# Hybrid attention / mLSTM step on one core: gate and up products of two FFN groups as float16 pairs

## The chip, the cores and the metric

The kernel runs on one core of one Trainium2 chip. The metric is the device time of one execution in microseconds; less is better. A core has five engines that run side by side, each through its own list in order: TensorE (PE, matmuls, with its weight loads shown as PEld), VectorE (DVE), ScalarE (ACT), GpSimd (POOL) and SyncE (SP, which here issues most DMA transfers). They wait for each other through semaphores. On-chip data lies in SBUF (128 partitions), sums of matmuls in the banks of PSUM.

## The reference

One layer over 1152 tokens (128 of a prompt, 1024 latent ones) of width 1024: grouped-query attention and a bidirectional mLSTM side by side, a joint output projection, then the part that is changed here, the feed-forward network (FFN):

```python
def swiglu(h, w_gu, w_down):
    g, u = jnp.split(h @ w_gu, 2, axis=-1)
    return (jax.nn.silu(g) * u) @ w_down
...
    h2 = rmsnorm(x, norm2_w) * (1 + sc2) + sh2
    x = x + g2 * swiglu(h2, w_gu, w_down)
```

`w_gu` is 1024 x 5632 (gate and up, 2816 columns each), `w_down` 2816 x 1024, all in float32. The shift `sh2`, scale `sc2` and gate `g2` come from a conditioning vector through `w_ada`.

## The kernel before

**Products of pairs.** A float32 product is made from three matmuls in a shorter format: each operand is split into an upper part (its rounding) and a lower part (what the rounding left), and high x high, high x low and low x high are summed in PSUM. The input projection `w_in` (class `Scaled`) does so with float16: since float16 has a small range, the operands are first multiplied by a power of two, found from a bound over all entries (`power_scale`: a PE transpose of a column of 128 bounds, a maximum on DVE, four small DVE operations on one number in `powers`, and a PE matmul that spreads the scale and its inverse to all partitions). The FFN and the output projection do it with fp32r, which needs no scale: `load_piece` (L139) loads 512 KB of weights into `raw` (two buffers), ACT casts the upper part into `whi` (L152), and `sub` (L137) makes the lower part `wlo` on DVE (five buffers each).

**Groups.** The 1152 tokens are nine blocks of 128, and the FFN runs over three groups of three blocks (384 tokens, `CT`), `c` = 0, 1, 2. In each, `gate_up` (L1316) goes over 4 or 5 of 22 column blocks `f`: for gate and for up it loads one weight piece, and `products` (L1310) makes 24 matmuls of 128 x 128 weights over 384 columns (8 steps of three, L1312 to L1314). From the two sums, `tn` = (tanh(g/2) + 1) u g on ACT and DVE (L1330 to L1332), which is split again into the pair `hl`. Then `down` (L1339) multiplies those by `w_down` in matmuls of 512 columns (L1112 to L1114) and adds to the rows `x1` (`add_gated`, L1098). The halving in the SiLU is folded into the gate `g2`.

**Beside the groups.** During groups 0 and 1, attention of the next group's blocks is woven in head by head: scores `S` (L1032, one buffer in PSUM), the row maximum on DVE (L1034), exp on ACT (L1035), a float16 pair of the probabilities (L1038, L1039), DMA transposes, and the products with the values (L1056, L1057). During the last `down` of a group, `norm2` (L1279) makes the pair `h2` = (`aTh`, `aTl`) of the next group: normalisation, PE transposes, scale and shift (L1301), a copy of the upper part (L1306) and `sub` for the lower one. The pair has one buffer each, b2 and b3, of six large ones.

**Order.** The loops write all instructions out once; a scheduler (`schedule_with_timeline_sim`) then orders them on each engine by its own simulated times. What the built program has in its lists is therefore not what the source order says. `prefill` (L1149), which runs ahead of group 0, adds the mLSTM half of the output projection to all rows; it waits for the rows `hm_d` that the last mLSTM head writes.

Of the kernel before, what the change touches and what calls it, by code (L numbers as in the profile page):

```python
# [8 lines left out]
F32 = mybir.dt.float32  # L9
F32R = mybir.dt.float32r  # L10
F16 = mybir.dt.float16
BF16 = mybir.dt.bfloat16
I32 = mybir.dt.int32
AF = mybir.ActivationFunctionType
ALU = mybir.AluOpType
# [4 lines left out]
P = 128  # L20
# [25 lines left out]
def hybrid_step(ctx: ExitStack, tc: tile.TileContext, I: dict, O: dict):  # L46
# [11 lines left out]
    def nm(s):  # L58
        uid[0] += 1
        return f"{s}_{uid[0]}"  # L60
# [10 lines left out]
    def emit(gen):  # L71
        for _ in gen:
            pass
# [62 lines left out]
    def sub(out, full, hi, eng):  # L136
        (dve if eng == "dve" else pool).tensor_tensor(out=out, in0=full, in1=hi, op=ALU.subtract)  # L137
# [28 lines left out]
    def power_scale(tp, one, bound, out):  # L166

        ps = bank()
        transpose(ps[0:1, 0:P], bound)
        v = tp.tile([1, 4], F32, name=nm("pv"), tag="pv", bufs=2)  # L170
        dve.tensor_reduce(out=v[:, 0:1], in_=ps[0:1, 0:P], axis=AX.X, op=ALU.max)
        powers(v, 1)
        yield
        ps = bank()
        mm(ps[:, 0:2], one, v[:, 2:4], start=True, stop=True)
        dve.tensor_copy(out, ps[:, 0:2])
        yield
# [55 lines left out]
    bcol = cp.tile([P, 48], F32, name="bcol")  # L233
    ncol = cp.tile([P, 16], F32, name="ncol")
    vsc = cp.tile([P, 4], F32, name="vsc")

    es_a = ExitStack()
    pA = es_a.enter_context(tc.tile_pool(name="pA", bufs=4, space=PSUM, reuse_waits="tile"))
# [835 lines left out]
    def a_tiles():  # L1074
        return (hp.tile([P, KD, CT], F32R, name=nm("aTh"), tag="b2"),
                hp.tile([P, KD, CT], F32R, name=nm("aTl"), tag="b3"))

    def new_x1(c):
        x1 = hp.tile([P, CB, D], F32, name=nm("x1"), tag=f"b{4 + c % 2}")
        for i in range(CB):  # L1080
            if c == 2:
                dma(x1[:, i, :], x1_d[i])
        return [x1[:, i, :] for i in range(CB)]
# [195 lines left out]
    def norm2(c, a, i):  # L1279

        x1 = a["x1"][i]
        if "h2" not in a:
            a["h2"] = a_tiles()
        th, tl = a["h2"]
        r = a["rs"][i]
        both = ap2.tile([P, KD, P], F32, name=nm("fl"), tag="pr", bufs=2)
        cnd = 0 if c * CB + i == 0 else 1
        for half in range(2):
            with hot(800):
                y = fp.tile([P, 512], F32, name=nm("y"), tag="y", bufs=2)  # L1290
                act(y, x1[:, half * 512 : (half + 1) * 512], AF.Copy, scale=r)
                ps = bank()
                for j in range(4):
                    transpose(ps[:, j * P : (j + 1) * P], y[:, j * P : (j + 1) * P])
                full = both[:, half * 4 : half * 4 + 4]
                for j in range(4):
                    k = half * 4 + j
                    if j == 0 and c == 0:
                        act(full[:, j, :], ps[:, j * P : (j + 1) * P], AF.Identity, scale=scale2[:, k, cnd : cnd + 1], bias=shift2[:, k, cnd : cnd + 1])
                        continue  # L1300
                    dve.tensor_scalar(  # L1301
                        out=full[:, j, :], in0=ps[:, j * P : (j + 1) * P],
                        scalar1=scale2[:, k, cnd : cnd + 1], scalar2=shift2[:, k, cnd : cnd + 1],
                        op0=ALU.mult, op1=ALU.add)
                oh = th[:, half * 4 : half * 4 + 4, i * P : (i + 1) * P]
                nc.scalar.copy(oh, full)  # L1306
                sub(tl[:, half * 4 : half * 4 + 4, i * P : (i + 1) * P], full, oh.bitcast(F32), "pool" if c == 0 else "dve")
            yield True

    def products(ps, wh, wl, th, tl):  # L1310
# [2 lines left out]
            mm(ps, wh[:, k, :], tl[:, k, :], start=False, stop=False)  # L1313
            mm(ps, wl[:, k, :], th[:, k, :], start=False, stop=(k == KD - 1))  # L1314

    def gate_up(a, f0, nf):  # L1316
        th, tl = a["h2"]
        acts = a["act"] = []
        for f in range(f0, f0 + nf):
            if True:  # L1320
                pg, pu = bank(), bank()
                for off, ps in ((0, pg), (D_FF, pu)):
                    src = w_gu[:, off + f * P : off + (f + 1) * P].rearrange("(k p) n -> p k n", p=P)
                    wh, wl = load_piece([(full_view, src)], (KD, P))
                    products(ps[:, 0:CT], wh, wl, th, tl)
                    yield 6
                parts = [(slice(0, CT), pg[:, 0:CT], pu[:, 0:CT])]
            tn = fp.tile([P, CT], F32, name=nm("tn"), tag="tn", bufs=2)
            for cs, g, u in parts:
                act(tn[:, cs], g, AF.Tanh, scale=0.5)  # L1330
                dve.scalar_tensor_tensor(out=tn[:, cs], in0=tn[:, cs], scalar=1.0, in1=u, op0=ALU.add, op1=ALU.mult)
                dve.tensor_tensor(out=tn[:, cs], in0=tn[:, cs], in1=g, op=ALU.mult)  # L1332
            hl = hlp.tile([P, 2, CT], F32R, name=nm("hl"), tag="hl", bufs=5)
            ah, al = hl[:, 0], hl[:, 1]
            nc.scalar.copy(ah, tn)  # L1335
            sub(al, tn, ah.bitcast(F32), "pool")
            acts.append((ah, al))
# [94 lines left out]
        ft.tile([P, 512], F32, name=f"lay_{tag}", tag=tag, bufs=bufs)  # L1432
    fp = ctx.enter_context(tc.tile_pool(name="fp", bufs=1, side="right", reuse_waits="tile"))

    cur, nxt = {}, {}
    cur["x1"], nxt["x1"] = new_x1(0), new_x1(1)
    es_x = ExitStack()
    xp = es_x.enter_context(tc.tile_pool(name="xp", bufs=1, side="right", reuse_waits="tile"))
    due = 0.0
# [8 lines left out]

    def groups(c, a, lst):
        for f0, nf in lst:  # L1450
            yield from gate_up(a, f0, nf)
            yield from down(c, a, f0, nf, 0)
            yield from down(c, a, f0, nf, 1)

# [10 lines left out]
    for c in range(NCH):  # L1465
        if c + 1 < NCH:
            main = groups(c, cur, GROUPS[:NG])
            for _ in range(4):
                next(main)
            weave(main, chain(previous(c, cur), att), 18 * sum(nf for _, nf in GROUPS[:NG]) - 24, 50)  # L1470
            emit(att)
            attn_out(nxt, oT, out_gates())
            emit(groups(c, cur, GROUPS[NG:-1]))
            f0, nf = GROUPS[-1]
            emit(gate_up(cur, f0, nf))
            n2 = chain(*[norm2(c + 1, nxt, i) for i in range(CB)])
            weave(chain(down(c, cur, f0, nf, 0), down(c, cur, f0, nf, 1)), n2, 6 * nf, 8)
            emit(n2)
            if c + 2 < NCH:
                oT = []  # L1480
                att = attention(c + 2, oT, set())
            nxt["prev"] = cur
            cur = nxt
            nxt = cur["next"] = {}
        else:
            main = groups(c, cur, LAST[:-1])
            for _ in range(4):
                next(main)
            weave(main, previous(c, cur), 24, 3)
            emit(main)  # L1490
            emit(gate_up(cur, *LAST[-1]))
            down_last(c, cur, *LAST[-1])


# [50 lines left out]
```

## Time and profile before

| | |
|---|---|
| median of three runs | 1588.04 us (1586.22 to 1590.58) |
| span of the profiled execution | 1590.3 us |
| PE busy | 1494.7 us (94%) |
| DVE busy | 1027.2 us (65%) |
| ACT busy | 768.8 us (48%) |
| POOL busy | 267.4 us (17%) |
| PE's mean granted clock | 0.978 |
| first and last gate/up product of group 0 | 632.9 and 933.1 us |
| of group 1 | 956.4 and 1278.6 us |
| of group 2 | 1301.9 and 1560.5 us |

The profile is of one execution. Its rows name the line, the engine, the operation, the output and the inputs with the program's names, shapes and types, the count, the busy time and the mean duration of one, and the idle time of the engine before them with what ended it. The profiler shows fp32r operands of PE as f32. PE's matmuls overlap each other, so their durations are longer than their distance; the distance is read from the starts in the timeline. The granted clock is a share of TensorE's full clock.

### The profile page before, as it was taken

The page shows a single profiled execution, that of the slowest core. Times are in us where ns is not written, and L with a number is a line of the kernel's source. Part 1 is how long each engine was busy: PE and PEld are TensorE (multiplying, and loading weights), DVE is VectorE, ACT ScalarE, POOL GpSimd, SP SyncE. Part 2 cuts the span into 40 slices and gives each one's busy share as a digit, 9 for nine tenths or more (in the row PEclk, how much of TensorE's full clock was granted, in tenths as well). Part 3 has the DMA queues.
Part 4 walks back from the last instruction along what each step waited for, and adds up shares of the span by engine and source line. Part 5 has one row for each costly group of instructions (what it writes and reads, how often), then busy time and mean ns, then how long its engine had stood idle before and what let it go on. Part 6 is the DMA issues. An engine that isn't in the chain of part 4 may idle for free.

```text
span 1590.3 us, 23425 instructions
## 1 busy us (share of the span) xinstructions
PE 1494.7 (94%) x8539; PEld 1249.4 (79%) x8539; DVE 1027.2 (65%) x2025; ACT 768.8 (48%) x1409; POOL 267.4 (17%) x357
## 2 busy tenths in 40 slices
PE   6799799999988679999999999999999999999996
PEld 3544467666766467888999999999898989999995
DVE  4778645755757576667654667877875575554555
ACT  4854365846656354535433435555552443323332
POOL 0023342332332243100110001000010101001111
PEclk9899899999999899999999999999999999999998
DMA  9474322432547746957754547968774445544441
GB/s 358 160 200 140 94 75 36 103 77 52 117 113 179 237 103 149 221 158 176 173 158 129 159 127 230 198 154 198 165 173 126 153 133 178 155 121 137 146 144 53
DMA packets 387881, 236.91 MB, mean 149 GB/s; under 512 B 170198, under 2 KB 346790, under 8 KB 387766
## 3 DMA queue, kind: packets, MB, share of 16 engines
q1 hardware_dynamic: 385110, 231.84, 54.0%
q10 hardware_dynamic: 2656, 3.58, 1.1%
q8 instruction: 67, 1.10, 0.3%
q14 instruction: 48, 0.39, 0.1%
HBM read 183.79 MB, written 13.26 MB: 124 GB/s over the span
## 4 chain that ended last, share of the span: by engine, by line
PE 75%; DVE 9%; DMA 8%; ACT 4%; issue 2%; SPq 1%; POOL 1%; ACTq 0%; DVEq 0%; POOLq 0%
PE mm L1313 11%; PE mm L1314 11%; PE mm L1312 11%; PE mm L1112 5%; PE mm L1113 5%; PE mm L1114 5%; PE S L1032 4%; PE wi L485 3%; PE wi L483 3%; PE wi L484 3%; PE mm L1144 1%; PE mm L1145 1%; DMA aw<-in_w_ada_dram 1%; PE po L1057 1%; PE po L1056 1%
## 5 line engine op out<-in xcount | busy, mean ns | idle before, releaser
L152 ACT CAST whi<-raw 128x1024 fp32r<-128x1024 f32 (+1 forms) x216 | 221.8, 1027 | 413.0 <-PE mm L1313 151.5
L137 DVE TENSOR_TENSOR wlo<-raw,whi 128x1024 fp32r<-128x1024 f32 (+1 forms) x216 | 260.5, 1206 | 203.8 <-ACT whi L152 203.2
L1313 PE MATMUL mm<-aTl,whi 128*128 128x384 f32 x1056 | 355.9, 337 | 2.7 <-DVE aTl L137 2.7
L1314 PE MATMUL mm<-aTh,wlo 128*128 128x384 f32 x1056 | 354.3, 335 | 0.0
L1312 PE MATMUL mm<-aTh,whi 128*128 128x384 f32 x1056 | 353.2, 336 | 0.0
L137 POOL TENSOR_TENSOR hl<-tn,hl 128x384 fp32r<-128x384 f32 x66 | 85.5, 1295 | 839.5 <-ACT hl L1335 721.3
L1313 PEld LDWEIGHTS mm<-aTl,whi 128*128 128x128 f32 x1056 | 198.5, 188 | 3.9 <-DVE aTl L137 3.3
L1312 PEld LDWEIGHTS mm<-aTh,whi 128*128 128x128 f32 x1056 | 198.1, 188 | 0.6
L1314 PEld LDWEIGHTS mm<-aTh,wlo 128*128 128x128 f32 x1056 | 198.4, 188 | 0.0
L1113 PE MATMUL mm<-wlo,hl 128*128 128x512 f32 x372 | 145.5, 392 | 0.0
L1112 PE MATMUL mm<-whi,hl 128*128 128x512 f32 x372 | 144.1, 392 | 0.0
L1114 PE MATMUL mm<-whi,hl 128*128 128x512 f32 x372 | 143.2, 392 | 0.0
L483 PE MATMUL wi<-ipair,hT 128*128 128x384 f16 (+2 forms) x408 | 136.2, 337 | 1.8 <-ACT hT L507 1.2
L484 PE MATMUL wi<-ipair,hT 128*128 128x384 f16 (+2 forms) x408 | 136.4, 337 | 0.0
L485 PE MATMUL wi<-ipair,hT 128*128 128x384 f16 (+2 forms) x408 | 132.5, 337 | 1.0 <-DVE hT L137 1.0
L1039 DVE SCALAR_TENSOR_TENSOR pl<-pr,st,ph 128x1152 f16<-128x1152 f32 (+1 forms) x72 | 93.8, 1303 | 33.8 <-ACT ph L1038 33.7
L1034 DVE TENSOR_REDUCE st<-S 128x1 f32<-128x1152 f32 (+1 forms) x72 | 88.9, 1235 | 14.6 <-PE S L1032 14.1
L1032 PE MATMUL S<-kst,qT 128*128 128x384 f32 (+1 forms) x400 | 87.6, 350 | 9.8 <-ACT pr L1035 5.6
L1035 ACT ACTIVATE pr<-S,st 128x1152 f32<-128x1152 f32 (+1 forms) x72 | 81.3, 1129 | 29.6 <-DVE st L1034 25.6
L1038 ACT ACTIVATE ph<-pr,st 128x1152 f16<-128x1152 f32 (+1 forms) x72 | 83.8, 1165 | 23.2 <-DVE st L1037 6.7
L1101 DVE TENSOR_TENSOR t<-mm,gl 128x512 f32<-128x512 f32 x102 | 68.9, 685 | 28.1 <-DMA gl<-g_d 10.2
L1032 PEld LDWEIGHTS S<-kst,qT 128*128 128x128 f32 x400 | 70.6, 191 | 14.7 <-ACT pr L1035 7.0
(366 smaller groups left out, 2539.7 us busy)
## 6 DMA issues: line engine op xcount, KB each, us to landing
raw<-in_w_gu_dram SPq DMA_DIRECT2D x132, 512.0 KB
raw<-in_w_down_dram SPq DMA_DIRECT2D x60, 512.0 KB
a<-in_w_ada_dram SPq DMA_DIRECT2D x24, 512.0 KB
gl<-g_d SPq DMA_DIRECT2D x36, 256.0 KB
aw<-in_w_ada_dram SPq DMA_DIRECT2D x16, 512.0 KB
iraw<-in_w_in_dram SPq DMA_DIRECT2D x32, 256.0 KB
raw<-in_w_out_dram SPq DMA_DIRECT2D x12, 512.0 KB
x<-in_x_sample_dram SPq DMA_DIRECT2D x11, 512.0 KB
```

The lines of the kernel that those rows point to most:

```text
L137: (dve if eng == "dve" else pool).tensor_tensor(out=out, in0=full, in1=hi, op=ALU.subtract)
L152: nc.scalar.copy(hi[:, :n], raw[:, :n])
L483: mm(ps[:, :n], ah, wh[:, k % 2, c0 : c0 + n], start=(k == 0), stop=False)
L484: mm(ps[:, :n], ah, wl[:, k % 2, c0 : c0 + n], start=False, stop=False)
L485: mm(ps[:, :n], al, wh[:, k % 2, c0 : c0 + n], start=False, stop=(k == KD - 1))
L1032: mm(S[:, n, 0:w], qT[:, h, :], kst[kv][:, t, c0 + n * w : c0 + (n + 1) * w], start=(t == 0), stop=(t == 1))
L1112: mm(ps, ah, wh[:, k % 2, :], start=(k == 0), stop=False)
L1113: mm(ps, ah, wl[:, k % 2, :], start=False, stop=False)
L1114: mm(ps, al, wh[:, k % 2, :], start=False, stop=(k == nk - 1))
L1312: mm(ps, wh[:, k, :], th[:, k, :], start=(k == 0), stop=False)
L1313: mm(ps, wh[:, k, :], tl[:, k, :], start=False, stop=False)
L1314: mm(ps, wl[:, k, :], th[:, k, :], start=False, stop=(k == KD - 1))
```

## The change

Group 0 stays with fp32r pairs. Groups 1 and 2 make gate and up from float16 pairs. Line numbers of the profile of before hold for the kernel before; the new functions are called by name.

- `bound_h2` (new, ahead of `prefill`) bounds |h2| by max|scale2| sqrt(1024) + max|shift2|, makes a power of two of it, and multiplies `scale2` and `shift2` by that for all three groups. `guc` holds the scales and inverses.
- `gate_piece` (new) loads a piece of `w_gu`. In group 0 it calls `load_piece` as before and sums |w| over each row of the piece on ACT (`AF.Abs` with an accumulator, 44 passes, its elementwise output `jg` is not used). In groups 1 and 2 it makes the float16 pair `wf`: ACT writes the upper half with the scale, DVE the lower one, both halves into one buffer, in turn of tag whi or wlo.
- `bound_w_gu` (new, behind the last `gate_up` of group 0) makes the power of two for `w_gu` from the largest row sum.
- The pair `h2` of groups 1 and 2 (`half_tiles`) takes one buffer, b3 for group 1 and b2 for group 2.
- tanh takes its scale, and the second gate operation the square of the inverse, from `guc`.
- The SBUF reserve for DMA descriptors is set to 256 bytes in a partition.

```diff
+    guc = cp.tile([P, 8], F32, name="guc")
+    gsum = cp.tile([P, 2 * NF], F32, name="gsum")
+    one2 = cp.tile([1, P], F32, name="one2")
+    dve.memset(one2, 1.0)
...
+    def half_tiles(c):
+        t = hp.tile([P, 2, KD, CT], F16, name=nm("hF"), tag=("b2", "b3")[c % 2])
+        return t[:, 0], t[:, 1]
...
-            a["h2"] = a_tiles()
+            a["h2"] = a_tiles() if c == 0 else half_tiles(c)
...
+    def gate_piece(c, i, src):
+        if c == 0:
+            raw = wp.tile([P, 1024], F32, name=nm("raw"), tag="raw", bufs=2)
+            jk = ft.tile([P, 1024], BF16, name=nm("jg"), tag="t2", bufs=3)
+            pieces = load_piece([(full_view, src)], (KD, P), raw=raw)
+            act(jk, raw, AF.Abs, accum_out=gsum[:, i : i + 1])
+            return pieces
+        raw = wp.tile([P, 1024], F32, name=nm("raw"), tag="raw", bufs=2)
+        w = wp.tile([P, 2, 1024], F16, name=nm("wf"), tag=("whi", "wlo")[i % 2], bufs=5)
+        dma(raw.rearrange("p (k n) -> p k n", k=KD), src)
+        hi, lo = w[:, 0], w[:, 1]
+        act(hi, raw, AF.Copy, scale=guc[:, 2:3])
+        dve.scalar_tensor_tensor(out=lo, in0=raw, scalar=guc[:, 2:3], in1=hi, op0=ALU.mult, op1=ALU.subtract)
+        return tuple(v.rearrange("p (k n) -> p k n", k=KD) for v in (hi, lo))
...
-                    wh, wl = load_piece([(full_view, src)], (KD, P))
+                    wh, wl = gate_piece(c, 2 * f + (off > 0), src)
...
-                act(tn[:, cs], g, AF.Tanh, scale=0.5)
+                act(tn[:, cs], g, AF.Tanh, scale=guc[:, 4:5])
...
-                dve.tensor_tensor(out=tn[:, cs], in0=tn[:, cs], in1=g, op=ALU.mult)
+                dve.scalar_tensor_tensor(out=tn[:, cs], in0=tn[:, cs], scalar=guc[:, 5:6], in1=g, op0=ALU.mult, op1=ALU.mult)
...
+    def bound_h2():
+        b2 = fp.tile([P, 2], F32, name="b2", tag="s1", bufs=3)
+        dve.tensor_reduce(out=b2[:, 0:1], in_=shift2, axis=AX.XY, op=ALU.max, apply_absolute_value=True)
+        dve.tensor_reduce(out=b2[:, 1:2], in_=scale2, axis=AX.XY, op=ALU.max, apply_absolute_value=True)
+        dve.scalar_tensor_tensor(out=b2[:, 1:2], in0=b2[:, 1:2], scalar=float(D) ** 0.5, in1=b2[:, 0:1], op0=ALU.mult, op1=ALU.add)
+        emit(power_scale(fp, one2, b2[:, 1:2], guc[:, 0:2]))
+        for t in (scale2, shift2):
+            dve.tensor_scalar(out=t, in0=t, scalar1=guc[:, 0:1], scalar2=None, op0=ALU.mult)
+        inverses_gu(guc[:, 1:2])
+    def inverses_gu(inv):
+        dve.tensor_scalar(out=guc[:, 4:5], in0=inv, scalar1=0.5, scalar2=None, op0=ALU.mult)
+        dve.tensor_tensor(out=guc[:, 5:6], in0=inv, in1=inv, op=ALU.mult)
+    def bound_w_gu():
+        b2 = fp.tile([P, 2], F32, name="b2w", tag="s1", bufs=3)
+        dve.tensor_reduce(out=b2[:, 0:1], in_=gsum, axis=AX.X, op=ALU.max)
+        emit(power_scale(fp, one2, b2[:, 0:1], guc[:, 2:4]))
+        dve.tensor_tensor(out=guc[:, 6:7], in0=guc[:, 1:2], in1=guc[:, 3:4], op=ALU.mult)
+        inverses_gu(guc[:, 6:7])
...
     cur["x1"], nxt["x1"] = new_x1(0), new_x1(1)
+    bound_h2()
...
-            emit(gate_up(cur, f0, nf))
+            emit(gate_up(c, cur, f0, nf))
+            if c == 0:
+                bound_w_gu()
...
-    nc = _bacc.Bacc("TRN2", target_bir_lowering=False, num_devices=1)
+    nc = _bacc.Bacc("TRN2", target_bir_lowering=False, num_devices=1, dynamic_dma_scratch_size=256)
```

More of the change, by code (lines that the diff above doesn't have):

```diff
@@ L1306, in norm2 @@
                 nc.scalar.copy(oh, full)
-                sub(tl[:, half * 4 : half * 4 + 4, i * P : (i + 1) * P], full, oh.bitcast(F32), "pool" if c == 0 else "dve")
+                sub(tl[:, half * 4 : half * 4 + 4, i * P : (i + 1) * P], full, oh.bitcast(F32) if c == 0 else oh, "pool" if c == 0 else "dve")
             yield True
@@ L1314, in products, with gate_up @@
             mm(ps, wl[:, k, :], th[:, k, :], start=False, stop=(k == KD - 1))
-    def gate_up(a, f0, nf):
+    def gate_piece(c, i, src):
[12 more added lines that the diff above has]
+        return tuple(v.rearrange("p (k n) -> p k n", k=KD) for v in (hi, lo))
+    def gate_up(c, a, f0, nf):
         th, tl = a["h2"]
@@ L1450, in groups @@
         for f0, nf in lst:
-            yield from gate_up(a, f0, nf)
+            yield from gate_up(c, a, f0, nf)
             yield from down(c, a, f0, nf, 0)
@@ L1490, in hybrid_step @@
             emit(main)
-            emit(gate_up(cur, *LAST[-1]))
+            emit(gate_up(c, cur, *LAST[-1]))
             down_last(c, cur, *LAST[-1])
```

## The prediction

> **What bounds the kernel now.** I read the busy times of five stretches first, then the list of PE's waits behind 632 us, where the FFN begins, then the timeline of PE for the pace of its matmuls.
>
> The columns after each stretch are its length, then busy time (and instructions) of PE, PEld, DVE, ACT and POOL, the granted clock, and the DMA share with GB/s:
>
> ```profile
> span 1590.3 us, 23425 instructions
> 200.00:500.00 300.00, 287.18 (x1863) 207.40 (x1862) 176.69 (x483) 191.34 (x539) 95.55 (x213) 0.98 0.41 88
> 632.00:956.00 324.00, 321.73 (x1751) 295.29 (x1750) 205.10 (x291) 139.97 (x183) 32.29 (x24) 1.00 0.61 163
> 956.00:1302.00 346.00, 344.96 (x1926) 318.04 (x1924) 256.28 (x379) 176.14 (x234) 27.29 (x22) 1.00 0.67 169
> 1302.00:1563.00 261.00, 259.37 (x1392) 245.84 (x1391) 140.53 (x185) 89.17 (x116) 28.41 (x22) 1.00 0.48 145
> 1563.00:1590.00 27.00, 14.22 (x63) 11.45 (x61) 16.98 (x54) 6.40 (x15) 4.67 (x4) 0.81 0.15 58
> ```
>
> The second, third and fourth rows are the three FFN groups. PE is busy for over 99% of each at full clock, while DVE stands at 63, 74 and 54% and ACT at 43, 51 and 34%. All of PE's waits from 632 us on:
>
> ```profile
> PE mm L1313 <- DVE aTl L137: 2.7, 2, 1.6
> PE po L1057 <- DMA plT<-pl: 1.3, 1, 1.3
> PE S L1032 <- ACT pr L1035: 1.0, 1, 1.0
> ```
>
> That is 5 us in 958. So PE bounds the FFN, and time that its matmuls give up there is time off the end, until something else is late.
>
> **Pace of the products.** First and last of 45 gate/up matmuls in a row (third group), then first and last of 24 float16 matmuls of the same 384 columns in the input projection. Columns: start, duration, line:
>
> ```profile
> 1399.82 0.33 PE L1312 MATMUL mm<-aTh,whi 128*128 128x384 f32 x1
> ...
> 1407.45 0.33 PE L1314 MATMUL mm<-aTh,wlo 128*128 128x384 f32 x1
> ...
> 316.30 0.33 PE L808 MATMUL wi<-hT,ipair 128*128 128x384 f16 x1
> ...
> 320.04 0.33 PE L810 MATMUL wi<-hT,ipair 128*128 128x384 f16 x1
> ```
>
> Durations overlap, so the starts count: 7.63 us over 44 steps is 173.4 ns; 3.74 us over 23 steps is 162.6 ns. Both stretches mix the three products in the same pattern. The weight loads under them and the matmuls by kind:
>
> ```profile
> L1312 PE MATMUL mm<-aTh,whi 128*128 128x384 f32 x1056 | 353.2, 336 | 0.0
> L1312 PEld LDWEIGHTS mm<-aTh,whi 128*128 128x128 f32 x1056 | 198.1, 188 | 0.6
> L808 PEld LDWEIGHTS <-ipair 128*128 128x128 f16 x96 | 10.1, 105 | 6.9 <-issue 2.2
> ```
>
> Each of the three products has 1056 matmuls, 352 a group, so the second and third group have 2112. All change. **Term 1: 2112 x (173.4 - 162.6) ns = 22.8 us less.**
>
> **A wait put between the first and second group.** `bound_w_gu` takes the maximum of the row sums: one PE transpose, a reduce on DVE, four small operations, one PE matmul that spreads the scale. In the built program's order PE has the transpose and this matmul directly behind the last gate/up product of the first group, ahead of the down products, and DVE has between them the last block's two gate operations and one lower half of a weight piece. Rows that price it:
>
> ```profile
> 933.50 0.56 DVE L1331 SCALAR_TENSOR_TENSOR tn<-tn,mm 128x384 f32<-128x384 f32 x1 [2.10 <-PE mm L1314]
> 934.09 0.55 DVE L1332 TENSOR_TENSOR tn<-tn,mm 128x384 f32<-128x384 f32 x1
> L171 DVE TENSOR_REDUCE pv<-mm 1x1 f32<-1x128 f32 x7 | 1.9, 277 | 4.2 <-PE mm L116 4.2
> L161 DVE TENSOR_SCALAR pv<-pv 1x1 f32<-1x1 f32 x7 | 1.0, 140 | 0.2
> L137 DVE TENSOR_TENSOR wlo<-raw,whi 128x1024 fp32r<-128x1024 f32 x204 | 252.3, 1237 | 183.7 <-ACT whi L152 183.1
> ```
>
> L1331 starts when the last product ends, at 933.50 in this trace; then 0.56 + 0.28 + 0.55 + 0.14 + 1.24 + 3 x 0.14 = 3.2 us, and 0.2 us from DVE to PE: PE stands for 3.4 us where it now goes on with the down products. Queued behind the waiting matmul are all of those. On DVE nothing is added ahead of the wait but the reduce. Such a stop can cost clock as well. Stretches with a long and a short wait in them, and what follows each:
>
> ```profile
> PE S L1032 <- DVE qT L137: 4.1, 1, 4.1
> 174.00:179.00 5.00, 0.91 (x6) 0.33 (x4) 3.83 (x13) 2.45 (x4) 0.00 (x0) 1.00 0.34 105
> 179.00:184.00 5.00, 4.95 (x21) 2.70 (x22) 3.11 (x8) 0.58 (x1) 3.06 (x2) 0.66 0.00 0
> 1302.00:1304.00 2.00, 0.53 (x4) 0.22 (x2) 2.00 (x3) 1.71 (x4) 0.00 (x0) 1.00 0.73 257
> 1304.00:1312.00 8.00, 7.83 (x45) 7.83 (x46) 7.11 (x20) 3.37 (x6) 0.00 (x0) 1.00 0.72 200
> 541.00:549.00 8.00, 6.85 (x18) 5.26 (x19) 3.25 (x4) 1.98 (x3) 0.00 (x0) 0.52 0.92 280
> PE mm L116 <- DMA t<-hm_d: 6.4, 1, 6.4
> ```
>
> After the 4.1 us wait the clock is 0.66 for 5 us (1.7 us lost); after 541 us, behind a wait of 6.4 us, 0.52 for 8 us (3.8 us lost); after the 1304 us stop of under 2 us, 1.00. The price lies between 0 and 3.8 us; I take 1.7, the nearest wait. **Term 2: +5.1 us, from 3.4 to 7.2.** The Trainium skill ("TensorE: Matmul & The Clock Gate", "Why this matters for your kernels") asks for no PE gaps over about 3 us between bursts, since one idle window halves the clock. The rows above bear it out; by that rule 3.4 us is at the edge, and without the clock loss the sum would be 1.7 us lower.
>
> **The scale of h2.** `bound_h2` stands ahead of the prefill: three DVE operations, a transpose, a reduce, four small ones, a matmul, a copy, two scalings of 16 columns, two of one column. PE's order puts its matmul ahead of the first transposes of the mLSTM rows, which wait for the load t<-hm_d today (the 6.4 us above). DVE also has one lower half of w_out in the chain. With L171 and L161 the DVE chain is some 2 us and that half 1.24, so between 0 (all under the load) and 3.3 us: PE's own matmuls there soon wait for the w_out pieces too. **Term 3: +1.5 us.** `dve.memset(one2)` is one row of 128 columns at the start, where PE waits for loads.
>
> **Row sums in the first group.** 44 ACT passes with their accumulator reads, priced by the same shape in the norm statistics, beside the passes that change:
>
> ```profile
> L1275 ACT ACTIVATE jk<-x 128x1024 bf16<-128x1024 f32 x15 | 15.8, 1054 | 2.7 <-DVE x L1102 1.8 <-POOL x L1102 0.8
> L1275 ACT ACTIVATION_READ_ACCUMULATOR jk<-x 128x1 f32 x15 | 2.8, 187 | 0.0
> L152 ACT CAST whi<-raw 128x1024 fp32r<-128x1024 f32 x204 | 214.3, 1051 | 379.5 <-PE mm L1313 138.6 <-DMA raw<-in_w_gu_dram 112.9 <-PE mm L1114 89.0
> L218 ACT ACTIVATE ipair<-iraw,isc 128x1024 f16<-128x1024 f32 x10 | 11.5, 1153 | 5.0 <-PE wi L485 4.9
> L219 DVE SCALAR_TENSOR_TENSOR ipair<-iraw,isc,ipair 128x1024 f16<-128x1024 f32 x10 | 13.0, 1304 | 6.4 <-ACT ipair L218 6.4
> L1035 ACT ACTIVATE pr<-S,st 128x1152 f32<-128x1152 f32 x64 | 78.4, 1225 | 22.7 <-DVE st L1034 21.9 <-DVE st L1037 0.3
> ```
>
> 44 x 1.241 = 54.6 us takes ACT from 140 to 195 us of 324 (60%): hidden behind PE on average. Not always: 12 heads of attention run in that stretch, one S buffer is freed by the exp on ACT, and a pass ahead of the exp delays the next head's S, with everything behind it on PE. From 0 to 12 x 1.24 = 14.9 us; PE waits 1.0 us for this now, so **Term 4: +2 us.** The junk output shares the t2 buffers with the gated adds, and a raw buffer is held one pass longer; the five weight buffers run ahead of PE and hide that.
>
> **Conversions in groups two and three.** Upper halves from 1.05 us (the cast, L152) to 1.153, lower ones from 1.237 to 1.304: 88 x 0.10 + 88 x 0.07 = 15 us over two engines with room. A pair takes half the buffer space, so more pieces lie ahead. The tight place is the second group: 24 heads, DVE 256 us, which becomes some 260 of 335 (78%). Bounds are 0 and 24 heads x half a lower half, 15.6 us; with DVE in no queue of PE's there now, **Term 5: +3 us.** The gate's second operation becomes a scalar_tensor_tensor, which L1331 shows at the same 0.55 us.
>
> **Order elsewhere.** The smaller descriptor reserve frees SBUF, and buffers that overlapped earlier ones no longer do: the built order moves the loads of the q/k tables ahead of eight loads of w_ada, and the key norms with them. The total of work is the same. The stretch in which they land:
>
> ```profile
> 100.00:200.00 100.00, 88.72 (x524) 45.09 (x523) 78.03 (x238) 43.36 (x86) 35.97 (x31) 0.93 0.44 134
> ```
>
> PE is idle there for 11 us, which a better order could win in part and a worse one add to; I take half on either side: **Term 6: 0, from -6 to +6 us.**
>
> **Sum.** -22.8 + 5.1 + 1.5 + 2 + 3 + 0 = -11.2 us. The profiled span of 1590.3 us lies 2.3 above the median of 1588.04; from the span it is 1579.1, from the median **1576.8**, forecast 1577. Its own range, by terms 2 to 6, is 1570 to 1583.
>
> **Rivals.**
> A, the gain whole: terms 3 to 5 hidden, the wait without loss of clock, 1588 - 22.8 + 3.4 = 1569, or a few less if the new order helps. For it: PE's 5 us of waits. Against: the fuller ACT and DVE. Chance 0.22.
> B, slower by the softmax chain: each S waits for an exp behind one ACT or DVE pass of about 1.2 us in more than the odd case. Of the 36 heads behind 632 us, 18 late ones cost 21.6 us: 1588 - 22.8 + 6.6 + 21.6 = 1593. It decides from 16.2 / 1.2 = 13 heads. For it: one S buffer, and the new program leaves only 5.3 us of PE work between some heads. Against: 1.0 us of such waits today. With half as many late heads it ends at 1583. Chance 0.14 for slower, 0.12 for the half.
> C, the pace stays: float16 streams no faster here, because something other than the weight load sets 173.4 ns. Then only terms 2 to 5 remain: 1588 + 11.6 = 1600. Against: the 162.6 ns over the same two streams. Chance 0.04.
> D, the weight load sets the pace: with 105 ns instead of 188 a matmul would come every 105 ns, 2112 x 68 ns = 144 us less, 1444. Against: the 162.6 ns with that very load. Chance 0.01. The Trainium skill (same page, "Back-to-back issue gap") gives about 131 ns for pairs of 512 columns; no row here shows it.
>
> **How the numbers follow.** The forecast has 0.47. What this kernel's measurement can tell from no change is 0.3%, 4.8 us, so faster means under 1583.3: forecast, A and D, 0.70. Within: the half of B and a part of the forecast's neighbours, 0.15. Slower: B and C with an unlucky term 6, 0.15. The range takes A with a good order (1563) and B (1593).
>
> **What would show it.** Starts of hF,wf products 162 to 163 ns apart; the second stretch shorter by 11 us less its new waits, the third group by 11.4; one PE wait of some 3.4 us for DVE pv just ahead of the down products of the first group, and the clock row behind it; PE S <- ACT pr summed from 632 us on, under 5 us. I am wrong if that last wait passes 15 us, if ACT whi waits turn into PE waits for pieces, or if the span before 632 us moves by over 6.

## The result, and the profile after

The changed kernel takes 1599.49 us (median of four runs, 1596.92 to 1601.65) against 1588.42 us for the kernel before beside it (1586.22 to 1590.58): a ratio of 1.0071, interval 1.0055 to 1.0087. That is 11.3 us slower, where 11.2 us faster was forecast, and outside the range. The profiled execution took 1599.78 us with a span of 1598.0 us.

Lengths by the first and the last gate/up product of each group, from the profiled executions:

| stretch | before, us | after, us | forecast of the difference |
|---|---|---|---|
| start to first product of group 0 | 632.9 | 621.3 | 1.5 (terms 3 and 6) |
| group 0 | 300.2 | 316.7 | 2 (term 4) |
| group 0 to 1 | 23.3 | 30.3 | 5.1 (term 2) |
| group 1 | 322.2 | 323.9 | -11.4 and a part of term 5 |
| group 1 to 2 | 23.3 | 24.2 | 0 |
| group 2 | 258.6 | 251.6 | -11.4 and a part of term 5 |
| behind it | 29.8 | 30.0 | 0 |

The differences add up to 7.7 us and not to 11.3, because the profiled execution of the kernel before was a long one: no other run of it on record has a span over 1589.9 us, and its own is 1590.3.

Some of the first two rows is only a shift: group 0 of the changed kernel holds 20 more matmuls of 512 columns (398 in place of 378), work of `prefill` that came later in the order. At 0.23 us each that is 4.7 us. So the start gained 7 us and group 0 lost 12. Busy times after, with the columns of the prediction's table of stretches:

```profile
621.00:938.00 317.00, 308.11 (x1658) 281.57 (x1657) 192.24 (x260) 178.19 (x258) 30.33 (x25) 0.99 0.61 160
938.00:968.00 30.00, 25.73 (x117) 20.72 (x117) 23.86 (x51) 14.19 (x19) 1.38 (x1) 0.94 0.41 123
968.00:1292.00 324.00, 315.48 (x1809) 220.76 (x1808) 234.85 (x337) 169.58 (x218) 24.88 (x21) 0.99 0.68 173
1316.00:1568.00 252.00, 247.81 (x1386) 163.94 (x1384) 141.10 (x185) 93.29 (x114) 24.26 (x21) 1.00 0.50 150
```

PE (its busy time against the length, first two numbers) idles 9 us in the first group, 4 in the step to the second, 8.5 in the second and 4 in the third; in the prediction's rows of the kernel before it was 5 us for all of them. In the second group DVE is busy for 72% and ACT for 52%, against 74 and 51% in the row of before: it isn't load that makes PE wait there. The longest of PE's waits from 621 us on, beside the list of the prediction (us in total, times, longest):

```profile
PE po L1060 <- DMA phT<-ph: 4.8, 4, 2.1
PE mm L175 <- DVE pv L164: 4.3, 1, 4.3
PE mm L1320 <- DVE tn L1355: 4.1, 2, 2.3
PE mm L1321 <- DVE hF L137: 3.0, 2, 2.3
PE mm L1322 <- DVE wlo L137: 2.8, 4, 0.8
PE S L1036 <- ACT pr L1039: 2.6, 4, 1.1
PE mm L1320 <- ACT whi L152: 2.1, 2, 1.7
```

The second row is the one that was forecast. The others are new or larger, and only 2.6 us of them are the softmax chain of rival B.

Short waits cost clock as well. In the prediction's rows of the kernel before, the clock is 1.00 in all three groups. The changed kernel has, beside the stretch behind the forecast wait (shown further down), three more at half clock:

```profile
642.90:646.30 3.40, 3.16 (x10) 3.16 (x11) 3.40 (x4) 3.40 (x5) 1.01 (x1) 0.50 0.54 153
987.70:991.10 3.40, 3.40 (x12) 1.64 (x11) 3.23 (x5) 0.73 (x3) 0.02 (x1) 0.50 0.88 275
1049.10:1052.50 3.40, 3.40 (x13) 2.54 (x10) 2.34 (x3) 1.03 (x1) 0.00 (x0) 0.50 0.86 211
```

They come at waits of 1.7 us (for whi, at 641.9 us), 2.3 us (for tn, at 987.2) and 2.1 us (for phT, at 1048.6). Each loses about 1.7 us, together some 5 us that no term of the prediction holds, and all three waits are shorter than the 3 us that it quotes as a limit. It isn't so behind every such wait: PE also waits 2.3 us for hF at 1319 us, and the clock stays full.

The pace of the float16 products came out as forecast. First and last of 240 in a row in the third group of the changed kernel (start, duration):

```profile
1380.88 0.34 PE L1320 MATMUL mm<-hF,wf 128*128 128x384 f16 x1
...
1419.73 0.33 PE L1322 MATMUL mm<-hF,wf 128*128 128x384 f16 x1
```

38.85 us over 239 steps is 162.6 ns. But products that the change doesn't touch became slower. First and last of 90 down products of 512 columns in the third group, before:

```profile
1407.62 0.39 PE L1112 MATMUL mm<-whi,hl 128*128 128x512 f32 x1
...
1427.84 0.39 PE L1114 MATMUL mm<-whi,hl 128*128 128x512 f32 x1
```

and the same products of the changed kernel:

```profile
1419.76 0.53 PE L1120 MATMUL mm<-whi,hl 128*128 128x512 f32 x1
...
1440.65 0.39 PE L1122 MATMUL mm<-whi,hl 128*128 128x512 f32 x1
```

20.22 us against 20.89 us over 89 steps, 227 against 235 ns. The three groups have 1188 of these. Some 0.1 us of the 0.67 is the first step behind float16 products; the rest, 6.4 ns a step, is no wait and no clock, since nearly all steps are longer and the median is 234 ns in each group, against 227. For 1188 products that is some 7.5 us.

### The profile page after: what moved, and what is told of

Read it like the earlier page. It is cut to its first block, busy times and chain, and to the rows that moved or that the text cites. A ratio compares the mean times of both kernels' runs of the same rounds, so it can differ in the third digit from the quotient of the medians.

```text
span 1598.0 us, 23425 instructions
## 1 busy us (share of the span) xinstructions
PE 1482.3 (93%) x8545; PEld 1094.3 (68%) x8545; DVE 1028.9 (64%) x2049; ACT 826.5 (52%) x1497; POOL 264.0 (17%) x357
## 5 line engine op out<-in xcount | busy, mean ns | idle before, releaser
L137 DVE TENSOR_TENSOR wlo<-raw,whi 128x1024 fp32r<-128x1024 f32 (+1 forms) x128 | 151.1, 1183 | 147.1 <-ACT whi L152 145.4
L1321 PE MATMUL mm<-hF,wf 128*128 128x384 f16 x704 | 230.5, 328 | 3.0 <-DVE hF L137 3.0
L1320 PE MATMUL mm<-hF,wf 128*128 128x384 f16 x704 | 229.3, 328 | 4.1 <-DVE tn L1355 4.1
L1322 PE MATMUL mm<-hF,wf 128*128 128x384 f16 x704 | 230.4, 328 | 0.0
L137 POOL TENSOR_TENSOR hl<-tn,hl 128x384 fp32r<-128x384 f32 x66 | 78.2, 1186 | 859.7 <-ACT hl L1359 791.4
L152 ACT CAST whi<-raw 128x1024 fp32r<-128x1024 f32 (+1 forms) x128 | 128.7, 1006 | 158.5 <-DMA raw<-in_w_down_dram 63.6
L1336 ACT ACTIVATE wf<-raw,guc 128x1024 f16<-128x1024 f32 x88 | 100.6, 1147 | 150.3 <-DMA raw<-in_w_gu_dram 132.4
L1337 DVE SCALAR_TENSOR_TENSOR wf<-raw,guc,wf 128x1024 f16<-128x1024 f32 x88 | 113.2, 1287 | 65.9 <-ACT wf L1336 65.6
L1322 PE MATMUL mm<-aTh,wlo 128*128 128x384 f32 x352 | 119.1, 339 | 2.8 <-DVE wlo L137 2.8
L1320 PE MATMUL mm<-aTh,whi 128*128 128x384 f32 x352 | 119.3, 339 | 2.1 <-ACT whi L152 2.1
L1321 PE MATMUL mm<-aTl,whi 128*128 128x384 f32 x352 | 118.6, 337 | 0.0
L1321 PEld LDWEIGHTS <-wf 128*128 128x128 f16 x704 | 69.2, 98 | 49.3 <-issue 6.1
L1322 PEld LDWEIGHTS <-wf 128*128 128x128 f16 x704 | 69.2, 98 | 48.6 <-issue 4.8
L1320 PEld LDWEIGHTS <-wf 128*128 128x128 f16 x704 | 69.1, 98 | 47.0 <-issue 2.9
```

What stands on the lines that cost most here:

```text
L152: nc.scalar.copy(hi[:, :n], raw[:, :n])
L1320: mm(ps, wh[:, k, :], th[:, k, :], start=(k == 0), stop=False)
L1337: dve.scalar_tensor_tensor(out=lo, in0=raw, scalar=guc[:, 2:3], in1=hi, op0=ALU.mult, op1=ALU.subtract)
```

## The experiments

Each run was timed beside the kernel before on the same chip, and ratios are against that. Addresses are the byte at which a buffer starts in a partition of SBUF, read from the built programs; the profile doesn't show them. The median steps are over all down products of a trace that follow each other.

### Where the buffers start

The change adds 720 bytes of constants (`guc`, `gsum`, `one2`) ahead of the weight buffers and small tiles ahead of `hl`. The first two runs move buffers and nothing else; PE's instructions stand in the same order.

e1:
```diff
     dve.memset(one2, 1.0)
+    cp.tile([P, 8], F32, name="pad")
```


> The changed kernel with an unused 32-byte column behind the new constants, so that all buffers behind them on that side start 0 instead of 96 bytes behind a multiple of 128; the order on every engine is the same. Theory address: the three new constants moved the buffers of weights, and the 512-column fp32r matmuls went from 227 to 234 ns for that. It expects starts 227 ns apart again and 1191 us (1189 to 1193) with a 1 put wrong here for 1591 us (1589 to 1593), 8 us less than the changed kernel. Rival mixture: fuller ACT and DVE, or the float16 matmuls between, slow them; it expects 234 ns and 1599 us (1598 to 1601) as before the pad.

Measured: 1588.53 us, ratio 1.0016 (0.9999 to 1.0034). The median step of the down products went from 234 to 229 ns. By its ratio the time is where the theory put it, the pace only partly: 5 of the 7 ns. For 1188 products 5 ns are some 6 us of the 8.7 us by which the ratio fell. The forecast stop is also shorter in e1's trace, 2.8 us in place of 4.3, and the two ratios leave 3 to 4 us open.

e2, the other way round, on the kernel before:
```diff
     vsc = cp.tile([P, 4], F32, name="vsc")
+    cp.tile([P, 24], F32, name="pad")
```


> The kernel before with an unused 96-byte column behind its constants, so that the same buffers start 96 bytes behind a multiple of 128; nothing else, and the same order. Theory address expects the 512-column fp32r matmuls 234 ns apart and 1597 us (1595 to 1599), 8 us more than the kernel before. Rival mixture expects 227 ns and 1588 us (1587 to 1590).

Measured: 1593.68 us, ratio 1.0043 (1.0027 to 1.0060), median step 232 ns. 96 unused bytes make the kernel before 6.8 us slower. The rival is out: there is no float16 gate/up product in it. What was left open is 227 against 229 in e1, where `hl` still lay off.

e5 moves `hl` to a multiple of 128 as well:
```diff
     fp = ctx.enter_context(tc.tile_pool(name="fp", bufs=1, side="right", reuse_waits="tile"))
+    fp.tile([P, 16], F32, name="pad2")
```


> The changed kernel with the 32-byte column of e1 and a second unused column of 64 bytes on the other side, so that hl (the stationary operand of the down products, 64 bytes behind a multiple of 128 in e1) starts at a multiple of 128 too; same order. Theory address, both operands: the 2 ns that e1 kept over the kernel before (229 to 227 ns) come from hl. It expects 227 ns and 1586 us (1584 to 1588). Rival: those 2 ns come from the float16 products between; it expects 229 ns and 1588.5 us (1587 to 1591).

Measured: 1591.20 us, ratio 1.0024 (1.0011 to 1.0037), median step 232 ns. Both were wrong: all buffers at multiples of 128, and the pace is worse than in e1. 64 bytes more on the side of `hl` changed it, so an address does it, but 128 isn't the unit. e9 below put `hl` on a multiple of 512; e11 and e12 then asked for the unit of each operand, on the kernel before.

e11:
```diff
     fp = ctx.enter_context(tc.tile_pool(name="fp", bufs=1, side="right", reuse_waits="tile"))
+    fp.tile([P, 64], F32, name="pad2")
```


> The kernel before with an unused 256-byte column ahead of hl alone, so that hl starts 256 bytes behind a multiple of 512 (0 in the kernel before); weights stay, same order. If the unit of the stationary operand is 256 bytes, the down products stay 227 ns apart and the time 1588 us (1586 to 1590). If it is 512, the row of one 128 x 128 fp32r tile, they take 229 to 233 ns and 1591 to 1595 us.

Measured: 1587.75 us, ratio 0.9993 (0.9983 to 1.0004). First and last of the 90 down products of the third group:

```profile
1402.12 0.39 PE L1112 MATMUL mm<-whi,hl 128*128 128x512 f32 x1
...
1422.33 0.39 PE L1114 MATMUL mm<-whi,hl 128*128 128x512 f32 x1
```

20.21 us, as before: 256 is enough for `hl`.

e12:
```diff
     vsc = cp.tile([P, 4], F32, name="vsc")
+    cp.tile([P, 32], F32, name="pad")
```


> The kernel before with an unused 128-byte column behind its constants, so that the weights start 128 bytes behind a multiple of 256 (0 in the kernel before); hl stays, same order. If the unit of the moving operand is 128 bytes (e2, 96 bytes off, broke it), 227 ns and 1588 us (1586 to 1590). If it is 256 as for hl, 229 to 233 ns and 1591 to 1595 us.

Measured: 1593.97 us, ratio 1.0034 (1.0023 to 1.0045), and the same 90 products:

```profile
1408.28 0.39 PE L1113 MATMUL mm<-whi,hl 128*128 128x512 f32 x1
...
1428.96 0.40 PE L1115 MATMUL mm<-whi,hl 128*128 128x512 f32 x1
```

20.68 us, 232 ns: 128 isn't enough for the weights either. Together (by their edits, e4 has the addresses of the changed kernel, e6 to e8 have those of e5, e10 has those of e9, and their median steps are the same):

| kernel | weights start at (modulo 256) | hl starts at (modulo 256) | median step, ns |
|---|---|---|---|
| before | 25856 (0) | 116224 (0) | 227 |
| e3 | 9728 (0) | 116224 (0) | 227 |
| e9 | 10496 (0) | 115712 (0) | 227 |
| e11 | 25856 (0) | 115968 (0) | 227 |
| e1 | 10496 (0) | 116160 (192) | 229 |
| e5 | 10496 (0) | 116096 (128) | 232 |
| e12 | 25984 (128) | 116224 (0) | 232 |
| e2 | 25952 (96) | 116224 (0) | 232 |
| after | 10464 (224) | 116160 (192) | 234 |

With both operands at multiples of 256 bytes the step is 227 ns, with either off it is 229 to 232, with both off 234. The pads move all buffers behind them on their side; that it is the two operands that count is read from the pace of these products, and no run moved the weights alone. The 384-column products don't show it: the fp32r ones of group 0 stay at 173 ns (aTh at 0 or 96 modulo 128), the float16 ones at 162 to 163.

### The reserve for descriptors alone

e3:
```diff
-    nc = _bacc.Bacc("TRN2", target_bir_lowering=False, num_devices=1)
+    nc = _bacc.Bacc("TRN2", target_bir_lowering=False, num_devices=1, dynamic_dma_scratch_size=256)
```


> The kernel before with only the reserve for DMA descriptors cut to 256 bytes; buffers stay at multiples of 128. Theory prefix: this alone gives the better order ahead of the first group that the changed kernel shows, worth about 7 us: 1581 us (1579 to 1584), with the first gate/up product some 12 us earlier than 632.9 us. Rival: the gain there came from what else the change moves (the scale of h2 among it), and the reserve alone gives 1588 us (1586 to 1591).

Measured: 1576.02 us, ratio 0.9935 (0.9921 to 0.9950): one line of the change makes the kernel before 10.3 us faster. The first gate/up product comes at 619.4 us, and everything behind it takes as long as before. Where the prediction's row of the kernel before shows 88.72 us of PE for 100 to 200 us, with 524 matmuls, e3 has

```profile
100.00:200.00 100.00, 94.79 (x585) 49.43 (x584) 70.01 (x228) 45.38 (x98) 33.16 (x36) 0.97 0.44 133
```

61 matmuls more fall into this stretch. In e3's order the loads of the q/k tables are issued at 46 us in place of 90 us; other loads moved too, and no run separates them. This is the gain at the start that the changed kernel shows, less what it lost again. It also means that the rest of the change is to be set against 1576 us, not 1588: it costs 1.0071 / 0.9935 = 1.4%, 22 us.

### Row sums in the first group

e4:
```diff
-            jk = ft.tile([P, 1024], BF16, name=nm("jg"), tag="t2", bufs=3)
             pieces = load_piece([(full_view, src)], (KD, P), raw=raw)
-            act(jk, raw, AF.Abs, accum_out=gsum[:, i : i + 1])
...
+    dve.memset(gsum, 32.0)
```


> The changed kernel without the 44 row-sum passes on ACT; the bound of w_gu is the constant 32 in their place (left out: the bound itself). Theory passes: they stand ahead of exp and of casts and cost the first group 6 to 8 us of PE waits; it expects 1592 us (1590 to 1594) and PE waits of under 4 us between 621 and 930 us, where the changed kernel has 8.9. Rival: the first group is longer only by the pace of its 512-column matmuls, and the sums are hidden: 1598 us (1597 to 1600).

Measured: 1590.13 us, ratio 1.0015 (1.0002 to 1.0028), 0.56% or 8.9 us less than the changed kernel. Group 0 falls from 316.7 to 309.5 us. PE's waits in it, after:

```profile
PE mm L1322 <- DVE wlo L137: 2.8, 4, 0.8
PE mm L1320 <- ACT whi L152: 2.1, 2, 1.7
PE po L1060 <- DMA phT<-ph: 2.1, 2, 1.2
PE S L1036 <- ACT pr L1039: 1.9, 2, 1.1
```

and without the sums:

```profile
PE S L1037 <- ACT pr L1040: 3.7, 2, 1.9
```

8.9 us against 3.7. What goes are the waits for the halves of the pieces (wlo and whi, 4.9 us) and for phT. The waits for the exp (pr) don't go, they rise from 1.9 to 3.7 us, so of the theory only the part on the casts is borne out. The built order changed in other places as well, and the stop behind the group is 2.8 us in place of 4.3. One place shows how a pass can get in the way, ACT at 635 us of the changed kernel (start, duration, and in brackets what ended the idle time before):

```profile
635.38 1.06 ACT L1330 ACTIVATE jg<-raw 128x1024 bf16<-128x1024 f32 x1 [4.32 <-DMA x_d<-t]
...
636.44 1.04 ACT L1330 ACTIVATE jg<-raw 128x1024 bf16<-128x1024 f32 x1
...
637.48 1.20 ACT L1039 ACTIVATE pr<-S,st 128x1152 f32<-128x1152 f32 x1
```

The first pass stands still for 4.3 us: its junk output takes a t2 buffer that a transfer to x_d must leave first. The exp behind it in ACT's list stands still too, and then waits out two passes. This doesn't make up the difference by itself: PE waits 3.5 us there up to 644 us, and without the passes it waits 3.7 us for two exps between 638 and 652 us.

### The scale of h2

e8 is e5 with `bound_h2` as two steps inside `prefill`:
```diff
-        emit(power_scale(fp, one2, b2[:, 1:2], guc[:, 0:2]))
+        steps = power_scale(fp, one2, b2[:, 1:2], guc[:, 0:2])
+        next(steps)
+        yield
+        emit(steps)
...
-    bound_h2()
...
-    for _ in prefill(cur, nxt):
+    h2 = bound_h2()
+    for i, _ in enumerate(prefill(cur, nxt)):
+        if i in (2, 4):
+            next(h2, None)
```


> e5 with the scale of h2 made in two steps inside prefill, after its first products, in place of ahead of it. Theory order: PE's 8.3 us wait for the bound delays prefill by about 5 us beyond what it would wait for anyway, and the half clock follows; it expects the first gate/up product 5 us earlier than in e5 and 1581 us (1579 to 1583). Rival: PE would wait there for the mLSTM rows and their pieces all the same: within 1.5 us of e5.

Measured: 1584.49 us, ratio 0.9982 (0.9970 to 0.9994), 0.42% or 6.7 us less than e5. PE around the first products of `prefill` in e5 (start, duration, wait):

```profile
529.46 0.37 PE L116 MATMUL mm<-ident,b 128*1 128x128 f32 x1 [7.83 <-DVE b L1466]
530.79 0.58 PE L175 MATMUL mm<-pv,one 1*128 1x2 f32 x2 [0.96 <-DVE pv L164]
531.30 1.12 PE L116 MATMUL mm<-ident,t 128*128 128x128 f32 x4
533.77 0.79 PE L1153 MATMUL mm<-whi,mx 128*128 128x512 f32 x1 [1.35 <-ACT mx L1190]
```

and in e8:

```profile
517.42 0.60 PE L116 MATMUL mm<-ident,t 128*128 128x128 f32 x4
...
528.17 0.79 PE L1153 MATMUL mm<-whi,mx 128*128 128x512 f32 x1 [7.15 <-ACT mx L1190]
```

PE waits about 7 us in both, which is what the rival said. But in e8 the four transposes of the mLSTM rows are done 11 us ahead, and their copy and lower half run under the wait; in e5 they stand behind the bound's transpose and come when it is over. The first product of e5 is 5.6 us later for that. Part of the gain is clock: from 515 us to the end of group 0 the clock is 0.50 for 27.3 us in e5 and for 20.5 us in e8. The first gate/up product does not come 5 us earlier, as the theory had it, but 2.3 us later (618.8 against 616.6 us): the 20 matmuls of `prefill` that e5 has in group 0 run ahead of it again. Group 0 falls from 315.8 to 307.1 us.

### The stop between the first two groups

The steps of the stop in the changed kernel:

```profile
938.16 0.27 PE L116 MATMUL mm<-ident,b2w 128*1 128x128 f32 x1
...
940.37 0.27 DVE L171 TENSOR_REDUCE pv<-mm 1x1 f32<-1x128 f32 x1
...
941.15 1.20 DVE L137 TENSOR_TENSOR wlo<-raw,whi 128x1024 fp32r<-128x1024 f32 x1
...
942.71 0.38 PE L175 MATMUL mm<-pv,one 1*128 1x2 f32 x2 [4.28 <-DVE pv L164]
```

and the granted clock behind it (the eighth column of the table of stretches):

```profile
943.30:946.70 3.40, 3.40 (x11) 2.82 (x10) 1.91 (x8) 1.34 (x2) 0.00 (x0) 0.50 0.52 154
```

4.3 us of stop and 3.4 us at half clock: 6.0 us in all. The four stretches at half clock behind 621 us start at 642.9, 943.3, 987.7 and 1049.1 us, 88, 13 and 18 times 3.41 us apart. The Trainium skill ("TensorE: Matmul & The Clock Gate", "What's actually happening") has the gate judge free-running windows of 3.4 us; the rows agree with it in length and distance. What a stop costs would then hang on where it falls among the windows, and the runs fit that: behind stops of 2.8 us e1 has 3.4 us at half clock and e4 6.8, behind stops of 4.2 us e8 has 3.4 and e5 6.8.

e6 is e5 with the second half of `bound_w_gu` later:
```diff
-            if c == 0:
-                bound_w_gu()
...
-            weave(chain(down(c, cur, f0, nf, 0), down(c, cur, f0, nf, 1)), n2, 6 * nf, 8)
+            d = chain(down(c, cur, f0, nf, 0), down(c, cur, f0, nf, 1))
+            if c == 0:
+                d = between(d, bound_w_gu(), (0, 3))
+            weave(d, n2, 6 * nf, 8)
```


> e5 with the matmul that spreads the scale of w_gu put 38 down matmuls (about 9 us) behind its transpose, in place of straight after it. Theory stop: PE's stop of 4.3 us and the half clock behind it go, 1580 us (1578 to 1582) against 1586 for e5, and the stretch between the last gate/up product of the first and the first of the second group falls from 28 to about 23 us. Rival: the pieces of the second group are then late, PE waits for them instead, and the time is that of e5 or more.

Measured: 1588.91 us, ratio 1.0003 (0.9990 to 1.0016), 3.3 us less than e5, about half of what was expected (the intervals overlap). The transition falls from 31.0 to 26.4 us, and the stop is replaced by waits behind it:

```profile
PE mm L1321 <- ACT hF L1315: 1.1, 1, 1.1
PE mm L1321 <- DVE t L1110: 1.1, 1, 1.1
PE mm L1321 <- DVE fl L1310: 1.0, 1, 1.0
```

and 6.8 us at half clock from 958 us. DVE is busy for 24.03 us of the 27 from 929 to 956 us: no piece of the second group can be converted before the scale is there, so conversions and the normalisation of h2 fall into the same 27 us. Neither theory had it whole.

### How far the conversions run ahead

e7 is e5 with a buffer for each half, so that the pieces lie five deep as before the change:
```diff
-        w = wp.tile([P, 2, 1024], F16, name=nm("wf"), tag=("whi", "wlo")[i % 2], bufs=5)
+        w = [wp.tile([P, 2, 1024], F16, name=nm("wf"), tag=t, bufs=5) for t in ("whi", "wlo")]
...
-        hi, lo = w[:, 0], w[:, 1]
+        hi, lo = w[0][:, 0], w[1][:, 0]
```


> e5 with the two halves of a float16 piece in a buffer of each tag, so that 5 pieces lie ahead as before the change and not 10. Theory depth: the deeper run-ahead puts conversions ahead of tanh and exp on ACT, and the waits of the second group (some 7 us: PE for tn, phT, plT) go with it: 1581 us (1579 to 1584), second group 314 us in place of 320. Rival: the waits come from the order of the attention chain and DVE's finish passes, whatever the depth: 1586 us (1584 to 1588), or more since less lies ahead.

Measured: 1581.88 us, ratio 0.9972 (0.9959 to 0.9985), 0.52% or 8.3 us less than e5. The second group falls from 320.8 to 313.5 us, the third from 251.0 to 248.9. PE's waits in both groups, e5:

```profile
PE po L1061 <- DMA phT<-ph: 3.7, 2, 2.1
PE mm L1322 <- DVE hF L137: 3.1, 2, 2.3
PE mm L1321 <- DVE tn L1356: 2.2, 1, 2.2
```

and e7:

```profile
PE S L1037 <- ACT pr L1040: 1.7, 1, 1.7
PE mm L1322 <- DVE hF L137: 1.6, 1, 1.6
PE po L1061 <- DMA phT<-ph: 0.8, 1, 0.8
PE mm L1321 <- DVE tn L1356: 0.2, 1, 0.2
```

Most of the waits for tn and phT go with the depth. With them go two stretches of 3.4 us at half clock (983.3 and 1311.0 us of e5), some 3.4 us of the 9.4 by which the two groups are shorter. Load isn't it: DVE is busy for 235 us of the group in both, ACT for 169 and 170. A likely way is that with half the buffer a piece, ten pieces could be converted as soon as they landed, in a row, and what stood behind them in the lists came late. The built order changed in other places too, so depth and order are not told apart.

### All of it mended

e9 is the changed kernel with e7 and e8, `hl` at a multiple of 512, and the scale of w_gu spread 15 matmuls behind its transpose (`hot` raises the priority of what it holds in the scheduler):
```diff
+    cp.tile([P, 8], F32, name="pad")
...
+    fp.tile([P, 112], F32, name="pad2")
...
+        with hot(800):
+            next(steps)
...
+                d = between(d, bound_w_gu(), (0, 2))
```


> The changed kernel with the 32-byte column, a second column of 448 bytes that puts hl at a multiple of 512 (the kernel before has it there), the two-slot halves of e7, the late scale of h2 of e8, and the scale of w_gu spread 15 matmuls behind its transpose. Theory address, finer: 128 isn't the unit, the pace follows the start modulo 256 of both operands (hl 0: 227, 192: 229, 128: 232 ns so far), and the down products are 227 ns apart. Rival: something other than these addresses sets it, 229 ns or more. Time: if the four costs are separate, 1591 for e5 less 9.3 (two slots), 6.7 (h2), 6 (pace) and 4 (stop) is 1565 us (1561 to 1570), below the 1576 of e3; if they share waits, 1573 to 1578.

Measured: 1566.59 us, ratio 0.9868 (0.9846 to 0.9890), and 227 ns. That is within 2 us of the sum of separate costs, and clear of the rival's 1573; each of the four costs is uncertain by 2 to 3 us itself. The 90 down products of the third group:

```profile
1387.04 0.53 PE L1121 MATMUL mm<-whi,hl 128*128 128x512 f32 x1
...
1407.37 0.39 PE L1123 MATMUL mm<-whi,hl 128*128 128x512 f32 x1
```

20.33 us, 0.11 more than before for the first step, and 0.56 less than in the changed kernel. The first transition of e9 and its third group:

```profile
925.00:949.00 24.00, 23.99 (x119) 19.55 (x118) 22.71 (x50) 11.40 (x16) 1.38 (x1) 1.00 0.44 132
...
1287.00:1534.00 247.00, 245.17 (x1381) 163.66 (x1379) 142.35 (x183) 93.83 (x115) 28.44 (x21) 1.00 0.51 153
```

The third group is 11.6 us shorter than before, as forecast for it, and PE no longer stops in the transition.

e10:
```diff
-            act(jk, raw, AF.Abs, accum_out=gsum[:, i : i + 1])
+            if i % 2:
+                dve.tensor_reduce(out=gsum[:, i : i + 1], in_=raw, axis=AX.X, op=ALU.max, apply_absolute_value=True)
+            else:
+                act(jk, raw, AF.Abs, accum_out=gsum[:, i : i + 1])
```


> e9 with every second row sum on ACT replaced by a row maximum of |w| on DVE (also a bound). Theory ACT's list: the sums cost by standing ahead of exp and casts on ACT, so half of them off ACT gives back half of the 9 us that e4 gained: 4 us less than e9. Rival: DVE's list is as tight in the first group, and the time is that of e9 within 2 us, or more.

Measured: 1564.11 us, ratio 0.9860 (0.9841 to 0.9879). The intervals of the two overlap: it isn't told apart from e9. In the profiled executions group 0 is 306.0 us against 309.0 in e9, but it begins 3.9 us later, and e9 has 6.8 us at half clock in it that e10 hasn't. Both beat the kernel before, and the reserve alone (e3).

## Why the prediction was wrong

**Term 1 (-22.8 us): right.** 162.6 ns, with 2112 products. Rivals C and D are out.

**Term 2 (+5.1): right in place and size.** 4.3 us and 1.7 us of clock; the order on DVE was the one read from the built program, with one more lower half in it. Of its 0.2 us from DVE to PE the trace shows under 0.1 (DVE's last step ends at 942.65, PE starts at 942.71).

**Not in the sum: +8 us for products that nobody touched** (0.56 us for each 90 of 1188 is 7.4, and the out-projection's have some more). This is the step that failed in kind. The change was worked out part by part by its instructions, and the three new constants were priced at one memset, that is at nothing. What they did was move the buffers behind them. e2 and e12 show it on the kernel before, at 6.8 and 5.4 us for the buffers on the weights' side. The Trainium skill ("SBUF — State Buffer", "Operand start alignment") asks only that an operand start at a multiple of its element size, and says that the runs behind this timed nothing; here the time depends on more.

**Term 6 (0, from -6 to +6): wrong in size.** -10.3 us by e3. The sum charged PE's 11 us of idle time from 100 to 200 us with half on either side, though the built order showed the loads that would fill it. Taken by itself, this hid the failure: without it the change would cost 22 us.

**Term 3 (+1.5, bound 3.3): wrong.** 6.7 us by e8. It was priced by the bound's own instructions and their cover, the wait for t<-hm_d. The new order loads those rows early, so that wait is gone, and what counted were the four transposes queued behind the bound, and the clock.

**Term 4 (+2, from 0 to 14.9): inside the bounds, mis-sized.** 8.9 us by e4. The prediction knew of a pass ahead of the exp, and waved away the junk output that shares t2 and the raw buffer held longer; the junk output held ACT for 4.3 us at 635 us, and it was the waits for whi and wlo that went without the passes, not those for the exp.

**Term 5 (+3, from 0 to 15.6): inside the bounds, mis-sized.** 8.3 us by e7. "More pieces lie ahead" was taken as harmless. e7 takes it back and gains this, depth and order together.

With the measured sizes: -22.8 - 10.3 + 8 + 6.0 + 6.7 + 8.9 + 8.3 = +4.8 us, against +11.3. Each difference of two ratios is uncertain by 2 to 3 us, so some 6 us of rest is no surprise, but it stays unassigned. The prediction priced half clock behind one stop alone; the 5 us behind short waits are partly in the differences of e4 and e7, so they aren't added here. e7 still has 4.3 us of PE waits in groups 1 and 2, a part of term 5 that is in no run's difference.

The range failed by itself too. The bounds of the terms add up to 1563 to 1612 us, which holds the measured time, and not to the 1570 to 1583 given for terms 2 to 6; the stated range ended at rival B's 1593, as if the costs couldn't come together. Rival B named the right sign with the wrong mechanism: PE waited 2.6 us for pr in all, not 21.6. That the time lies at rival C's 1600 is chance, since the pace, its mechanism, came out as forecast. Of the marks set beforehand two came true: PE waited for whi and wlo of pieces in group 0, and the span ahead of 632 us moved by more than 6.

Open are: what in the reading of operands costs the 2 to 7 ns, and whether products of a smaller type over 512 columns show it.

## What to carry to other kernels

Price the storage that a change takes, not only its instructions: compare the start addresses of every hot operand in both built programs, and pad constants to a multiple of 256 bytes. Where a new step waits, look at what is queued behind it and would have run under a wait that exists already; and where a transfer or conversion may run further ahead, ask whose place in an in-order list it takes. Run each line of a change by itself: here one line was worth 10 us and the others hid it.

## What the hardware showed unexpectedly

- 128x128 by 512-column fp32r matmuls follow each other at 227 ns when both operands start at multiples of 256 bytes in a partition, and at 229 to 234 ns at the other addresses of the table; kernels with the same addresses have the same median step. 384-column ones show no difference (173 ns).
- Waits of 1.7 to 2.3 us can have 3.4 us at half clock behind them (642.9, 987.7 and 1049.1 us of the changed kernel), and a stop of 2.8 us can have as much behind it as one of 4.2 (6.8 us in e4 and e5).
